# Sums of weight blocks by accumulating DMAs in place of VectorE, in a one-core hybrid attention and recurrence block

## The chip, the cores and the metric

The kernel runs on one core of a Trainium2 chip. The metric is device time in microseconds: the time of one launch of the whole program. The engines are named as the profile names them: PE is TensorE's matmul, PEld its loading of weights, DVE is VectorE, ACT is ScalarE, POOL is GpSimd and SP is SyncE. DMAs are started from the queue of SP (in a few places of ACT) and from the queue of POOL. Each queue runs its instructions in order.

## The reference

One layer of a decoder block on a sequence of 1024 tokens with 1024 channels, all in float32: a modulated RMSNorm, one wide input projection, two branches (sliding-window attention with 16 heads and 4 key heads, and a gated linear recurrence behind a short convolution), a gated merge of the two, an output projection, the residual and a last RMSNorm. Cut to what matters here:

```python
h = rmsnorm(x, norm_g[l]) * (1.0 + scale[:, None, :]) + shift[:, None, :]
proj = h @ w_in[l]
q, k, v, g_attn, xr, g_rnn, m_attn, m_rnn = jnp.split(proj, SPLIT_POINTS, axis=-1)
...
y_attn = sliding_window_attention_with_sinks(q, k, v, attn_sinks[l]) * jax.nn.silu(g_attn)
xr = causal_depthwise_conv(xr, conv_w[l], conv_b[l])
y_rnn = rg_lru(xr, positions, ...) * jax.nn.silu(g_rnn)
merged = (jax.nn.sigmoid(m_attn) * (y_attn @ w_attn_proj[l])
          + jax.nn.sigmoid(m_rnn) * (y_rnn @ w_rnn_proj[l]))
x = x + gate[:, None, :] * (merged @ w_out[l])
```

The change concerns `h @ w_in`, the largest product.

## The kernel before

**Precision.** Every float32 operand of a matmul is split in two float32r parts, a high part (a rounded copy, made on ACT) and a low part (what is left, made on DVE); a product is then three matmuls: high times high, low weight times high, high weight times low. In the names, `wh` and `wl` are the two parts of a block of weights, `hh`, `hl` those of the activations h, `nh`, `nl` those of differences of activations.

**Seven products for eight.** The output columns of `w_in` are cut in chunks of 128 and taken in 22 pairs of chunks (class `Pair`, line 700). The weights of a pair are four blocks of 128 by 512 numbers in memory: A11, A12 (first chunk, the two halves of the 1024 input channels) and A21, A22 (second chunk). The 2 by 2 block product is done with seven block products by Strassen's method in Winograd's form. It needs four sums of weight blocks: S1 = A21 + A22, S2 = S1 - A11, S3 = A21 - A11 and S4 = S2 - A12. S2 is made from S1 and S4 from S2. The other side needs four sums of activation blocks, made once (`differences`, line 563, then split by `make_operands`, line 571). Each product is 12 matmuls of 128 by 128 by 512 (`product`, line 691).

**Slots.** `run` (line 818) emits the products in slots. Pair i has its first slot at s = 7i; the products of a pair come at s (A11), s+1 (S1), s+3 (S2), s+4 (A12), s+5 (S4), s+6 (S3) and s+9 (A22, in the place between S1 and S2 of the next pair). Behind the product of slot t stand the steps that were put down for t in a table (`at_slot`, line 676): loads, sums, high parts (`hi`), low parts (`lo`), copies out of the accumulators and what is done with the results (the `sinks`). The background work (the gates of the recurrence, the preparation of `w_out` and so on) is fitted in between by `background` (line 653), with estimated costs of each step on ACT and DVE. The order on each engine is fixed when the program is built.

**Before the first pair** the steps of slots -6 to 0 are emitted at three places by hand (`begin`, lines 1559, 1578 and 1581), among the steps that finish the operands of the activations.

**Around the change, per pair.** At s-6 to s-4 SP loads A11 and A21, A22 and A12. The high and low parts and the four sums (`tsum`, line 715, on DVE) are put at s-2 to s+5; S1 at s-2, S2 at s-1, S3 at s, S4 at s+2. A22's parts follow at s+7. C11, C12, C21 and C22, the four result blocks, go to the sinks at s+5 to s+11: rotary embedding for q, a tanh for the gates, the convolution for the recurrence.

**POOL's queue** holds, in this stretch, only DMAs that prepare `w_out`: `out_weights` (line 1168) loads blocks `wq`, DVE multiplies and subtracts them, and POOL stores them to `wq_d`. When the last pair but one is nearly done, the attention is opened (`open_attn`, line 1234): SP loads keys, queries and the sinks of the softmax, POOL copies a column of the sinks into the first tile of scores, loads values, and from then on also stores the tanh results (`smr_d`) and does the masks. The last pair runs between the first steps of attention.

Of the kernel before, what the change touches and what calls it, by code (L numbers as in the profile page):

```python
# [22 lines left out]
P = 128  # L23
S = 1024
# [28 lines left out]
def tile_hybrid_block(ctx, tc, x, x_t, pk, rows, posr, posi, c_row, w_ss, w_gate, w_main, w_v,  # L53
# [8 lines left out]
    def f32(ap):  # L62
        return ap.bitcast(F32)
# [497 lines left out]
    NT1, NT3, NT4, T2 = [], [], [], []  # L561

    def differences(i):
# [3 lines left out]
        V.tensor_tensor(out=b12_, in0=b12_, in1=b22, op=ALU.subtract)  # L567
        V.tensor_tensor(out=b22, in0=b22, in1=b11, op=ALU.add)
        V.tensor_tensor(out=b21, in0=b21, in1=b22, op=ALU.subtract)

    def make_operands(i):
# [5 lines left out]
        NT3.append((nh[i][:, SL[1]], nl[i][:, SL[1]]))  # L577
        NT4.append((nh[i + 4][:, SL[0]], nl[i + 4][:, SL[0]]))
        T2.append((nh[i + 4][:, SL[1]], nl[i + 4][:, SL[1]]))
# [41 lines left out]
    def rope_b(src, th, dst, r0=P):  # L621
        t = {}

        def f1():
            t["h"] = rpp.tile([P, HALF], F32R, tag="rh", name="rhi", bufs=2)
            A.copy(t["h"][:], src())

        def f2():
            t["l"] = rpp.tile([P, HALF], F32R, tag="rl", name="rlo", bufs=2)
            V.tensor_tensor(out=t["l"][:], in0=src(), in1=f32(t["h"][:]), op=ALU.subtract)  # L630
# [69 lines left out]
    class Pair:  # L700
# [3 lines left out]
        def place(self, s, par, last, put_):  # L704
# [4 lines left out]

            def load(n):  # L710
                i, j = int(n[1]) - 1, int(n[2]) - 1
                return "S", 0, 0, lambda: R.__setitem__(
                    n, load_half(w_main[self.c + i][:, SL[j]]))

            def tsum(dst, a, b, op):
                def f():
                    R[dst] = wp.tile([P, HALF], F32, tag="ws", name="ws", bufs=3)[:]
                    V.tensor_tensor(out=R[dst], in0=R[a], in1=R[b], op=op)
                return "D", 0, 0.69, f
# [7 lines left out]
            def lo(n):  # L727
                return "D", 0, 0.69, lambda: rest(O[n], R[n], sc)

            SUB, ADD = ALU.subtract, ALU.add  # L730
            at_slot(s - 6, [load("A11"), load("A21")], load("A22"), load("A12"))
            put_(s - 2, [hi("A11"), tsum("S1", "A21", "A22", ADD)],
                 [hi("S1"), lo("A11"), tsum("S2", "S1", "A11", SUB)],
                 [lo("S1"), tsum("S3", "A21", "A11", SUB)],
                 hi("S2"),
                 [hi("A12"), lo("S2"), tsum("S4", "S2", "A12", SUB)],
                 [hi("S4"), lo("A12")], [hi("S3"), lo("S4")], lo("S3"))
            at_slot(s + (5 if last else 7), hi("A22"), lo("A22"))
# [14 lines left out]
            def join(out_, n, a, b):  # L753
# [1342 lines left out]
```

## Time and profile before

| what | before |
|---|---|
| time, three runs | 912.44, 913.25, 914.01 us; median 913.25 |
| profiled execution, span from first to last instruction | 910.2 us (its time outside the span is not recorded) |
| granted TensorE clock, mean | 0.997 |
| PE busy | 892.0 us, 98% of the span |
| DVE busy | 722.1 us, 79% |
| ACT busy | 557.6 us, 61% |
| POOL busy | 125.2 us, 14% |
| bytes moved by DMA | 182.05 MB, mean 200 GB/s |
| sums of weight blocks on DVE (line 718) | 88 of 128x512, 60.2 us in all |

The pairs run from 112 us to about 584 us of the span. Before that are the norm, the first products and the operands; after it the rest of the attention, the projections of the two branches, the merge and the output projection. A matmul of 128x512 is shown as 389 ns long, but matmuls are pipelined and one starts every 0.227 us, so that a slot of 12 is 2.73 us. Busy time of PE is the time in which at least one is under way.

### The profile page before, as it was taken

The numbers are of one execution on the slowest core, as the hardware profiler recorded it, in microseconds if no ns is written. First come the engines' busy times: TensorE is split into PE (matmuls) and PEld (weight loads), VectorE is DVE, ScalarE is ACT, GpSimd is POOL, SyncE is SP. The second block draws the span as 40 slices with busy tenths as digits, with TensorE's granted clock in tenths as the row PEclk, the third lists the DMA queues.
The fourth block names the chain that finished last, engine by engine and source line by source line (L and its number), as shares of the span: only waits on it lengthen the run. The fifth ranks groups of instructions, "written<-read, shape, count | busy, mean of one in ns | idle before, by whom it ended". The sixth has DMA issues, their size and how long they took to land.

```text
span 910.2 us, 12609 instructions
## 1 busy us (share of the span) xinstructions
PE 892.0 (98%) x4187; PEld 740.7 (81%) x4187; DVE 722.1 (79%) x1143; ACT 557.6 (61%) x1088; POOL 125.2 (14%) x204
## 2 busy tenths in 40 slices
PE   5999999999999999999999999999999999999997
PEld 3879888887888788888887888888888888888886
DVE  7976889797679983988498576899999946779875
ACT  6753655454566755775678685888888731114555
POOL 0120000000010010000000001354444421310002
PEclk9999999999999999999999999999999999999998
DMA  9963458862344362346155257996666259878314
GB/s 351 414 212 110 163 168 312 281 230 85 116 144 151 116 234 86 115 151 225 36 197 166 84 192 253 338 368 215 203 199 219 93 172 330 306 273 322 140 46 185
DMA packets 88598, 182.05 MB, mean 200 GB/s; under 512 B 13891, under 2 KB 30275, under 8 KB 88534
## 3 DMA queue, kind: packets, MB, share of 16 engines
q1 hardware_dynamic: 81908, 161.57, 51.0%
q0 software_dynamic: 6336, 19.37, 5.9%
q8 instruction: 33, 0.54, 0.2%
q14 instruction: 31, 0.25, 0.1%
q10 hardware_dynamic: 290, 0.32, 0.1%
HBM read 124.49 MB, written 57.12 MB: 200 GB/s over the span
## 4 chain that ended last, share of the span: by engine, by line
PE 87%; DVE 5%; DMA 4%; ACT 2%; issue 1%; POOL 0%; SPq 0%; DVEq 0%; ACTq 0%
PE bk L696 43%; PE rp L174 13%; PE bo L1869 7%; PE pmain L174 6%; PE pgate L991 5%; PE bk L174 3%; PE s_ps L1283 3%; PE pv L1355 2%; DMA r<-w_main 2%; PE pt L1321 1%; DVE wl L110 1%; PE bk L1529 1%; PE bk L1528 1%; PE bk L1527 1%; DMA wada<-w_ss 1%
## 5 line engine op out<-in xcount | busy, mean ns | idle before, releaser
L696 PE MATMUL bk<-nh,wl 128*128 128x512 f32 x352 | 137.4, 390 | 0.4 <-DVE wl L110 0.4
L696 PE MATMUL bk<-nh,wh 128*128 128x512 f32 x352 | 137.1, 389 | 0.0
L696 PE MATMUL bk<-nl,wh 128*128 128x512 f32 x352 | 137.0, 389 | 0.0
L110 DVE TENSOR_TENSOR wl<-r,wh 128x512 fp32r<-128x512 f32 x113 | 80.5, 727 | 7.4 <-ACT wh L104 7.4
L104 ACT CAST wh<-r 128x512 fp32r<-128x512 f32 x113 | 68.6, 618 | 21.6 <-PE bk L1529 12.2
L60 POOL DMA_DIRECT2D wq_d<-wq x32 | 22.0, 687 | 423.7 <-DVE wq L1181 379.3
L696 PEld LDWEIGHTS bk<-nh,wl 128*128 128x128 f32 x352 | 66.1, 188 | 15.1 <-DVE wl L110 1.5
L696 PEld LDWEIGHTS bk<-nh,wh 128*128 128x128 f32 x352 | 66.1, 188 | 13.8
L696 PEld LDWEIGHTS bk<-nl,wh 128*128 128x128 f32 x352 | 66.1, 188 | 13.6
L696 PE MATMUL bk<-hh,wl 128*128 128x512 f32 x176 | 68.6, 390 | 0.4 <-DVE wl L110 0.4
L696 PE MATMUL bk<-hh,wh 128*128 128x512 f32 x176 | 68.6, 390 | 0.0
L696 PE MATMUL bk<-hl,wh 128*128 128x512 f32 x176 | 68.5, 389 | 0.0
L110 DVE TENSOR_TENSOR wl<-ws,wh 128x512 fp32r<-128x512 f32 x76 | 51.7, 683 | 0.0
L1307 ACT ACTIVATE p<-p,small 128x129 f32<-128x129 f32 x128 | 50.1, 401 | 0.0
L104 ACT CAST wh<-ws 128x512 fp32r<-128x512 f32 x76 | 45.8, 614 | 0.1
L1869 PE MATMUL bo<-wh,sum 128*128 128x512 f32 x128 | 39.6, 389 | 0.0
L696 PEld LDWEIGHTS bk<-hh,wh 128*128 128x128 f32 x176 | 33.0, 188 | 7.7 <-ACT wh L104 0.9
L696 PEld LDWEIGHTS bk<-hh,wl 128*128 128x128 f32 x176 | 33.0, 188 | 7.5 <-DVE wl L110 0.8
L696 PEld LDWEIGHTS bk<-hl,wh 128*128 128x128 f32 x176 | 33.0, 188 | 6.9
L1283 PE MATMUL s_ps<-ks,qs 128*128 128x256 f32 (+1 forms) x256 | 37.6, 289 | 0.2 <-DVE p L1297 0.2
L799 ACT ACTIVATE c<-bk 128x512 f32<-128x512 f32 x29 | 17.3, 597 | 30.2 <-PE bk L696 30.2
L696 PE MATMUL bk<-hha,wl 128*128 128x512 f32 x88 | 34.5, 392 | 0.6 <-DVE wl L110 0.5
(412 smaller groups left out, 2336.7 us busy)
## 6 DMA issues: line engine op xcount, KB each, us to landing
r<-w_main SPq DMA_DIRECT2D x100, 256.0 KB, 4.3
wada<-w_ss SPq DMA_DIRECT2D x16, 512.5 KB, 9.0
qs<-q_d SPq DMA_DIRECT2D x16, 512.0 KB, 5.8
wq_d<-wq POOLq DMA_DIRECT2D x24, 256.0 KB, 4.6
wr<-wq_d SPq DMA_DIRECT2D x24, 256.0 KB, 5.0
ks<-k_d SPq DMA_DIRECT2D x24, 192.0 KB, 5.0
wq<-w_out POOLq DMA_DIRECT2D x16, 256.0 KB, 5.7
q_d<-rhi SPq DMA_DIRECT2D x16, 256.0 KB, 4.1
```

Source lines behind the costliest of these rows:

```text
L60: return eng.dma_start(dst, src)
L104: A.copy(dst[0][:], src)
L110: V.tensor_tensor(out=dst[1][:], in0=src, in1=f32(dst[0][:]), op=ALU.subtract)
L174: mm = T.matmul(ps[hf], ww, xx[kc][hf], start=(kc == 0 and ww is w_h and xx is xh), stop=(kc == KC - 1 and xx is xl))
L696: W["pe"] = T.matmul(ps, ww[:, c], b[kc][xx_], start=(first and kc == 0 and i == 0), stop=(kc == 3 and i == 2), skip_group_check=not first)
L799: A.activation(t["t"], s(), AF.Tanh, scale=0.5)
L991: W["pe"] = T.matmul(ps[:, SL[hf]], ww[:, c0:c0 + P], xx_[:, SL[hf]], start=(ic == 0 and i == 0), stop=(ic == 1 and i == 2))
L1283: W["pe"] = T.matmul(o, qs[:, j, qc], ks[:, b, k0 + (0 if n else P):k0 + 256], start=(b == 0), stop=(b == 1))
L1307: A.activation(px[:, j, :], px[:, j, :], AF.Exp, bias=sm[:, 0, j:j + 1], accum_out=sm[:, 1, j:j + 1])
L1321: W["pe"] = T.transpose(pt[:, j, :], px[:, j, 0:P], ident[:])
L1355: W["pe"] = T.matmul(pv[:], b, m[:].rearrange("p j q -> p (j q)"), start=(i == 0), stop=(i == len(prods) - 1))
L1869: T.matmul(bank[p][i] if dst is None else dst, a[:, ts_], b[:][:, sl], start=(new and kc == 0 and j == 0), stop=(kc == 3 and j == 2), skip ...
```

## The change

The four sums of a pair are made by DMAs that add what they read to what lies in the tile (`accum_op=ALU.add`), started from POOL's queue, `grow` in the diff. One tile X of the pool `ws` takes, one after the other, A21 (a plain load), then + A22 (this is S1), + A11 (S2), + A12 (S4). The tile that held A11 takes + A21 and becomes S3. Since a DMA can add but not subtract, the sums stand with the other sign where it was a difference: with -A21, -A22 as the second chunk's blocks all four sums are what the method needs times -1. Three of the four sums of activations are therefore taken with the other sign too, and the results of the second chunk come out negative and are turned in the sinks (a scale of -1 in an instruction that was there anyway).

Each block is now read from memory by each DMA that adds it: eight transfers of 256 KB per pair in place of four. A DMA that adds to X waits until the high and the low part of what X held have been made. The steps stand at other slots: A21 is loaded at s-8, S1 is made at s-6, A11 is loaded at s-6, A12 at s-2, A22 at s+3; S1's high part is at s-3 and its low part at s-2, with S2's DMA behind it; S2's parts at s and s+1, with S4's DMA behind; S4's parts at s+3 and s+4.

```diff
@@ -558,15 +558,17 @@
...
-    NT1, NT3, NT4, T2 = [], [], [], []
+    NT1, T3, T4, NT2 = [], [], [], []
 
     def differences(i):
         b11, b12_ = xT[i][:, SL[0]], xT[i][:, SL[1]]
         b21, b22 = xT[i + 4][:, SL[0]], xT[i + 4][:, SL[1]]
         V.tensor_tensor(out=b11, in0=b11, in1=b12_, op=ALU.subtract)
-        V.tensor_tensor(out=b12_, in0=b12_, in1=b22, op=ALU.subtract)
-        V.tensor_tensor(out=b22, in0=b22, in1=b11, op=ALU.add)
-        V.tensor_tensor(out=b21, in0=b21, in1=b22, op=ALU.subtract)
+        V.tensor_tensor(out=b12_, in0=b22, in1=b12_, op=ALU.subtract)
+        V.scalar_tensor_tensor(out=b22, in0=b22, scalar=-1.0, in1=b11, op0=ALU.mult,
+                               op1=ALU.subtract)
+        V.scalar_tensor_tensor(out=b21, in0=b22, scalar=-1.0, in1=b21, op0=ALU.mult,
+                               op1=ALU.subtract)
 
     def make_operands(i):
         for t in (i, i + 4):
...
@@ -618,16 +620,20 @@
         return [("AD", 1.16, 0.69, f1), ("D", 0, 1.38, f2)] + rope_b(
             lambda: t["ra"], th, dst, 0)
 
-    def rope_b(src, th, dst, r0=P):
+    def rope_b(src, th, dst, r0=P, sign=1.0):
         t = {}
 
         def f1():
             t["h"] = rpp.tile([P, HALF], F32R, tag="rh", name="rhi", bufs=2)
-            A.copy(t["h"][:], src())
+            if sign > 0:
+                A.copy(t["h"][:], src())
+            else:
+                A.activation(t["h"][:], src(), AF.Copy, scale=sign)
 
         def f2():
             t["l"] = rpp.tile([P, HALF], F32R, tag="rl", name="rlo", bufs=2)
-            V.tensor_tensor(out=t["l"][:], in0=src(), in1=f32(t["h"][:]), op=ALU.subtract)
+            V.scalar_tensor_tensor(out=t["l"][:], in0=src(), scalar=sign, in1=f32(t["h"][:]),
+                                   op0=ALU.mult, op1=ALU.subtract)
             dma(dst[r0:r0 + P, SL[th]], t["h"][:])
             dma(dst[r0 + 2 * P:r0 + 3 * P, SL[th]], t["l"][:])
 
@@ -707,16 +713,22 @@
             R, O, sc = {}, {}, self.scale
             self.ops, self.banks = O, (b1, b2, b3, bk[2 - par])
 
+            def part(n):
+                i, j = int(n[1]) - 1, int(n[2]) - 1
+                return w_main[self.c + i][:, SL[j]]
+
             def load(n):
-                i, j = int(n[1]) - 1, int(n[2]) - 1
-                return "S", 0, 0, lambda: R.__setitem__(
-                    n, load_half(w_main[self.c + i][:, SL[j]]))
-
-            def tsum(dst, a, b, op):
+                return "S", 0, 0, lambda: R.__setitem__(n, load_half(part(n)))
+
+            def begin_sum():
+                R["X"] = wp.tile([P, HALF], F32, tag="ws", name="ws", bufs=3)[:]
+                dma(R["X"], part("A21"))
+
+            def grow(dst, t, n):
                 def f():
-                    R[dst] = wp.tile([P, HALF], F32, tag="ws", name="ws", bufs=3)[:]
-                    V.tensor_tensor(out=R[dst], in0=R[a], in1=R[b], op=op)
-                return "D", 0, 0.69, f
+                    G.dma_start(R[t], part(n), accum_op=ALU.add)
+                    R[dst] = R[t]
+                return "N", 0, 0, f
 
             def hi(n):
                 def f1():
@@ -727,15 +739,19 @@
             def lo(n):
                 return "D", 0, 0.69, lambda: rest(O[n], R[n], sc)
 
-            SUB, ADD = ALU.subtract, ALU.add
-            at_slot(s - 6, [load("A11"), load("A21")], load("A22"), load("A12"))
-            put_(s - 2, [hi("A11"), tsum("S1", "A21", "A22", ADD)],
-                 [hi("S1"), lo("A11"), tsum("S2", "S1", "A11", SUB)],
-                 [lo("S1"), tsum("S3", "A21", "A11", SUB)],
-                 hi("S2"),
-                 [hi("A12"), lo("S2"), tsum("S4", "S2", "A12", SUB)],
-                 [hi("S4"), lo("A12")], [hi("S3"), lo("S4")], lo("S3"))
-            at_slot(s + (5 if last else 7), hi("A22"), lo("A22"))
+            def early(t, *steps):
+                at_slot(max(t, -6), *steps)
+
+            ADD, SUB, MUL = ALU.add, ALU.subtract, ALU.mult
+            early(s - 8, ("S", 0, 0, begin_sum))
+            early(s - 6, [grow("S1", "X", "A22"), load("A11")])
+            at_slot(s - 2, load("A12"))
+            at_slot(s + (1 if last else 3), load("A22"))
+            put_(s - 3, hi("S1"), [lo("S1"), grow("S2", "X", "A11"), hi("A11")],
+                 [lo("A11"), grow("S3", "A11", "A21")])
+            put_(s, hi("S2"), [lo("S2"), grow("S4", "X", "A12")], hi("A12"),
+                 [lo("A12"), hi("S4")], [lo("S4"), hi("S3")], lo("S3"))
+            at_slot(s + (5 if last else 7), [hi("A22"), lo("A22")])
 
             T_ = {}
 
@@ -750,17 +766,18 @@
             at_slot(s + 4, keep("u2", b2))
             at_slot(s + 5, *self.sinks["C11"](lambda: b1))
 
-            def join(out_, n, a, b):
+            def join(out_, n, a, b, sign=1.0):
                 def f():
                     T_[n] = out_()
-                    V.tensor_tensor(out=T_[n], in0=a(), in1=b(), op=SUB)
+                    V.scalar_tensor_tensor(out=T_[n], in0=a(), scalar=sign, in1=b(), op0=MUL,
+                                           op1=ADD if sign > 0 else SUB)
                 return "D", 0, 0.69, f
 
             d12, k12 = self.sinks["C12"]
             d22, k22 = self.sinks["C22"]
             at_slot(s + 6, join(d12, "C12", lambda: T_["u2"][:], lambda: b3),
                     *k12(lambda: T_["C12"]))
-            at_slot(s + 7, join(d22, "C22", lambda: b2, lambda: T_["p5"][:]),
+            at_slot(s + 7, join(d22, "C22", lambda: b2, lambda: T_["p5"][:], -1.0),
                     *k22(lambda: T_["C22"]))
             if last:
                 def add():
@@ -773,7 +790,7 @@
     def rope_q(g):
         return {"C11": lambda s: rope_a(s, 0, q_d[g]), "C12": (blk, lambda s: rope_a(
                     s, 1, q_d[g])),
-                "C21": lambda s: rope_b(s, 0, q_d[g]), "C22": (blk, lambda s: rope_b(
+                "C21": lambda s: rope_b(s, 0, q_d[g], sign=-1.0), "C22": (blk, lambda s: rope_b(
                     s, 1, q_d[g])), "late": 11}
 
     behind = []
@@ -790,24 +807,24 @@
             behind.pop(0)()
 
     def tanh_sinks(dst, silu):
-        def steps(j, th):
+        def steps(j, th, sign=1.0):
             def sink(s):
                 t = {}
 
                 def f1():
                     t["t"] = blk()
-                    A.activation(t["t"], s(), AF.Tanh, scale=0.5)
+                    A.activation(t["t"], s(), AF.Tanh, scale=0.5 if silu else 0.5 * sign)
                     if not silu:
                         dma(dst[j][:, SL[th]], t["t"], G if "att" in W else nc.sync)
 
                 def f2():
-                    V.scalar_tensor_tensor(out=t["t"], in0=t["t"], scalar=1.0, in1=s(),
+                    V.scalar_tensor_tensor(out=t["t"], in0=t["t"], scalar=sign, in1=s(),
                                            op0=ALU.add, op1=ALU.mult)
                     store(dst[j][:, SL[th]], t["t"])
 
                 return [("A", 0.62, 0, f1)] + ([("D", 0, 0.69, f2)] if silu else [])
             return sink
-        return {"C11": steps(0, 0), "C12": (blk, steps(0, 1)), "C21": steps(1, 0),
+        return {"C11": steps(0, 0), "C12": (blk, steps(0, 1)), "C21": steps(1, 0, -1.0),
                 "C22": (blk, steps(1, 1))}
 
     def place(pairs):
@@ -821,11 +838,11 @@
         for t in range(-6, 7 * n + 14):
             i, k = divmod(t, 7)
             q = {0: (0, "A11", B11, 1, True), 1: (0, "S1", NT1, 2, True),
-                 2: (-1, "A22", NT4, 1, False), 3: (0, "S2", T2, 1, False),
+                 2: (-1, "A22", T4, 1, False), 3: (0, "S2", NT2, 1, False),
                  4: (0, "A12", B21, 0, False), 5: (0, "S4", B22, 2, False),
-                 6: (0, "S3", NT3, 1, False)}[k]
+                 6: (0, "S3", T3, 1, False)}[k]
             if t == 7 * n:
-                q = -1, "A22", NT4, 3, True
+                q = -1, "A22", T4, 3, True
             d = 0.0
             if 0 <= i + q[0] < n and t <= 7 * n:
                 d = extra()
@@ -865,7 +882,8 @@
             return xr[ic]
 
         def copy(ic):
-            return lambda s: [("A", 0.58, 0, lambda: A.copy(row(ic)[:, SL[0]], s()))]
+            return lambda s: [("A", 0.58, 0, lambda: A.activation(
+                row(ic)[:, SL[0]], s(), AF.Copy, scale=-1.0 if ic else 1.0))]
 
         def half(ic):
             return lambda: row(ic)[:, SL[1]]
```

**How instructions move.** PE runs the same matmuls; those of the gates stand a few products earlier, since the planner counts DVE as freer. DVE loses the 88 sums, POOL gains 88 DMAs. Three places matter for the prediction.

On ACT, ahead of the first pair. `wh` from `r` is the high part of A11, `wh` from `ws` that of a sum, `nh` are high parts of activations, the `c` from `bk` are tanh results. Before:

```order
L106 ACTIVATE wh_1188<-r_1068 128x512
L1571 ACT_TABLE_LOAD
L1571 ACTIVATE c_1193<-bk2_70 128x512
L1571 ACTIVATE c_1196<-bk3_71 128x512
L574 CAST nh2_772<-xT_201 128x1024
L574 CAST nh6_773<-xT_205 128x1024
L106 ACTIVATE wh_1205<-ws_1191 128x512
L574 CAST nh3_770<-xT3_202 128x1024
L574 CAST nh7_771<-xT7_206 128x1024
```

and in the change, from the same place:

```order
L106 ACTIVATE wh_1185<-ws_1068 128x512
L106 ACTIVATE wh_1192<-r_1071 128x512
L1589 ACT_TABLE_LOAD
L1589 ACTIVATE c_1195<-bk2_70 128x512
L1589 ACTIVATE c_1198<-bk3_71 128x512
L576 CAST nh2_772<-xT_201 128x1024
L576 CAST nh6_773<-xT_205 128x1024
L106 ACTIVATE wh_1211<-ws_1068 128x512
L576 CAST nh3_770<-xT3_202 128x1024
L576 CAST nh7_771<-xT7_206 128x1024
```

S1's high part now stands ahead of A11's; the high part from `ws_1068` in the second place, between `nh6` and `nh3`, is S2's, which before was S1's (S2's came behind `nh7` and two more).

On SP, where the attention is opened. `ks`, `qs` and `sink` are its first loads, `smr_d` a store of a tanh result, `r` a load of weights. Before:

```order
L60 DMA r_5067<-w_main 128x512
L60 DMA smr_d4_118<-c_5103 128x512
L60 DMA ks_5129<-k_d_87 64x2x256 x2
L60 DMA qs_5132<-q_d0_98 128x4x256
L60 DMA sink_5126<-rows 128x16
L60 DMA ks_5136<-k_d_87 64x2x384 x2
```

and in the change:

```order
L60 DMA r_4981<-w_main 128x512
L60 DMA smr_d3_117<-c_5018 128x512
L60 DMA r_5021<-w_main 128x512
L60 DMA ks_5039<-k_d_87 64x2x256 x2
L60 DMA qs_5042<-q_d0_98 128x4x256
L60 DMA sink_5036<-rows 128x16
L60 DMA ks_5046<-k_d_87 64x2x384 x2
```

Before, the first load of keys stood behind the store of the first result of pair 21 of 22 (`smr_d4`, slot 145); now it stands behind the last result of pair 20 (`smr_d3`, slot 143), two slots earlier.

On POOL, at the same hand-over. `yh_d`, `yl_d` are the last results of the recurrence, `p` from `sink` is the first tile of scores, `dv` and `vs` are values. Before:

```order
L60 DMA yh_d7_129<-yh_5111 128x1024
L60 DMA yl_d7_137<-yl_5114 128x1024
L1271 COPY p_5127<-sink_5126 128x4
L60 DMA dv_5142<-dv_d0_93 128x256
L60 DMA vs_5141<-vs_d0_89 128x128
L60 DMA smr_d4_118<-c_5180 128x512
L60 DMA smr_d5_119<-c_5201 128x512
L1300 AFFINE_SELECT p_5127<-p_5127 128x4x128
```

and in the change, from the same `yh_d`, where `ws` and `r` from `w_main` are sums of the last pair:

```order
L60 DMA yh_d7_129<-yh_4983 128x1024
L60 DMA yl_d7_137<-yl_4986 128x1024
L1289 COPY p_5037<-sink_5036 128x4
L60 DMA dv_5052<-dv_d0_93 128x256
L60 DMA vs_5051<-vs_d0_89 128x128
L60 DMA smr_d4_118<-c_5089 128x512
L729 DMA ws_4933<-w_main 128x512
L729 DMA r_4981<-w_main 128x512
L60 DMA smr_d4_118<-c_5131 128x512
L60 DMA smr_d5_119<-c_5151 128x512
L729 DMA ws_4933<-w_main 128x512
L1318 AFFINE_SELECT p_5037<-p_5037 128x4x128
```

The DMAs that make S2 and S3 of the last pair stand behind the copy of the sinks, two loads of values and one store; S4's behind two stores more, and the mask of the first scores behind S4's.

6 lines of the change are left out of this document (3 added, 3 removed).

## The prediction

> **What bounds the kernel now.** I read three views first: busy time by engine, busy time by stretch, and PE's waits. Behind the times of the windows stand the number of instructions, then the granted clock, the DMA engines' mean busy share and GB/s.
>
> ```profile
> PE 892.0 (98%) x4187; PEld 740.7 (81%) x4187; DVE 722.1 (79%) x1143; ACT 557.6 (61%) x1088; POOL 125.2 (14%) x204
> core 0: us, PE busy (x) PEld busy (x) DVE busy (x) ACT busy (x) POOL busy (x), PEclk, DMA share, GB/s
> 45.00:112.00 67.00, 66.49 (x382) 58.25 (x381) 49.07 (x72) 35.02 (x55) 5.18 (x10) 1.00 0.47 168
> 112.00:566.00 454.00, 452.63 (x1989) 371.56 (x1989) 356.75 (x510) 291.73 (x426) 16.89 (x27) 1.00 0.48 165
> 566.00:896.00 330.00, 329.64 (x1633) 277.26 (x1632) 270.04 (x457) 192.18 (x539) 97.64 (x155) 1.00 0.67 232
> PE bk L387 <- DVE xt L381: 7.0, 1, 7.0
> PE bk L696 <- DVE wl L110: 1.3, 3, 0.5
> 112.27 106.17 PE bk L696 x467
> ```
>
> From 45 to 896 us PE is busy for 66.49 + 452.63 + 329.64 of 851 us: 2.2 us are idle. DVE's 79% is busy time beside it, not ahead of it. The largest wait (7.0 us) is at line 387, before the pairs, where the change touches nothing. The last row is from the chain of waits: 467 of the pairs' matmuls in 106.17 us without a break, so one takes 0.2273 us and a slot of 12 takes 2.73 us.
>
> **The change part by part.**
>
> *Removed: 88 sums on DVE.* From the groups by line:
>
> ```profile
> L718 DVE TENSOR_TENSOR ws<-r 128x512 f32<-128x512 f32 x44 | 30.1, 685 | 1.9 <-DMA r<-w_main 1.9
> L718 DVE TENSOR_TENSOR ws<-ws,r 128x512 f32<-128x512 f32 x44 | 30.1, 684 | 0.0
> ```
>
> 60.2 us of DVE go. PE can gain only where it waits for DVE: 1.3 us in three waits for low parts in the pairs (line 110). I count half, -0.6, since each such low part also needs a high part from ACT, which is relieved of nothing. Bounds: 0 and -1.3.
>
> *Added: 88 accumulating DMAs on POOL's queue.* No row shows such a DMA. What matters is L, the time from its issue to its landing, since each sum waits for the one before it. The nearest rows are POOL's own transfers (medians; the `wq` rows are from the windows 200 to 300, 300 to 400 and 400 to 500 us, `smr_d` and `yl_d` from 545 to 600; then the tile `wq` over the whole span), beside SP's load of the same block:
>
> ```profile
> r<-w_main SPq DMA_DIRECT2D x100, 256.0 KB, 4.3
> wq<-w_out POOLq DMA_DIRECT2D x2, 256.0 KB, 4.3
> wq<-w_out POOLq DMA_DIRECT2D x2, 256.0 KB, 5.9
> wq<-w_out POOLq DMA_DIRECT2D x2, 256.0 KB, 5.1
> smr_d<-c POOLq DMA_DIRECT2D x7, 256.0 KB, 6.4
> yl_d<-yl POOLq DMA_DIRECT2D x1, 512.0 KB, 7.5
> L60 POOL DMA_DIRECT2D wq_d<-wq x32: 565/727/744, 263.0 to 804.7; - x32
> DMA to landing us min/median/max: 2.0/4.7/9.4
> ```
>
> A load of 256 KB takes 4.3 to 5.9 us here. An accumulating one also reads its destination, so I take the largest, L = 5.9, for the pairs, and 6.4 where the attention opens. Bounds: 4.3 (the second stream costs nothing) and 7.5 (as much as 512 KB). The 22.5 MB more, over 454 us, add 50 GB/s to 165, still below the 232 of the next stretch. POOL's issues cost 88 times 0.73 = 64 us of an engine that has 16.89 busy in 454: hidden.
>
> The Trainium skill, "DMA: Bandwidth & Descriptors", section "Anatomy of one DMA — SWDGE (gpsimd) path", fits such a DMA by 2.0 us and its bytes at 436 GB/s; for 256 KB that is an estimate of 2.6 us. The trace's 4.3 to 5.9 do not agree, and no run here shows an accumulating one. By the page every loss below would vanish but the 0.3 of the first pair's low part, and the time would be 913.0.
>
> *The first pair.* It has no run-up. ACT's and DVE's timelines:
>
> ```profile
> 105.26 0.63 ACT L106 ACTIVATE wh<-r 128x512 fp32r<-128x512 f32 x1
> 108.17 2.00 ACT L574 CAST nh<-xT 128x1024 fp32r<-128x1024 f32 x2
> 110.59 2.00 ACT L574 CAST nh<-xT 128x1024 fp32r<-128x1024 f32 x2
> 113.44 0.65 ACT L106 ACTIVATE wh<-ws 128x512 fp32r<-128x512 f32 x1
> 106.00 0.69 DVE L718 TENSOR_TENSOR ws<-r 128x512 f32<-128x512 f32 x1
> 109.25 2.36 DVE L575 TENSOR_TENSOR nl<-xT,nh 128x1024 fp32r<-128x1024 f32 x2 [2.57 <-ACT nh L574]
> 111.53 0.68 DVE L112 SCALAR_TENSOR_TENSOR wl<-r,wh 128x512 fp32r<-128x512 f32 x1
> ```
>
> S1's high part now stands ahead of A11's on ACT: 0.63 later for the `nh` behind them, for the `nl` on DVE and for A11's low part at 111.53, which then ends at 112.84. PE takes the high parts first and wants it some 0.23 into the product, at 112.50: 0.34 late.
>
> The chain of sums: S1's low part takes the place of the sum at 106.00 and ends at 106.7. S2's DMA lands at 106.7 + 5.9 = 112.6; its high part (0.65) ends at 113.25. Ahead of its low part stand two `nh` (2.0) on ACT and the second `nl` half (1.2) on DVE: 116.45, and 117.1 with it. S4's DMA lands at 123.0, high part 123.65, low part 124.35. S4's product is the fifth: it starts at 112.27 + 0.34 + 4 x 2.73 = 123.5 and wants the low part at 123.75: 0.6 late. Together 0.9. Bounds: 0.34 at L = 4.3, and 0.3 + 3.8 = 4.1 at 7.5, since two transfers of the chain count.
>
> *The pairs between.* High parts of successive sums stand three slots apart, 8.2 us. Less a high part (0.65 us) and a low part (0.68) there remain 6.9 for L and for waiting in DVE's order: 5.9 fits, so nothing is lost. How far it may grow: from S1's high part (behind the product of slot s-3) to S4's product (s+5) are seven slots, 19.1 us. Three high parts and two low parts take 3.3, and of S4's low part 0.45 must lie ahead of the product; 15.4 remain for two transfers. So the loss starts at about L = 7.7 and is 2 x (L - 7.7) a pair beyond. This term is 0 at both bounds of L.
>
> *The hand-over to the attention.* From the timelines of SP, POOL, ACT and DVE and, for the last five rows, the chain of waits around 566 us:
>
> ```profile
> 555.76 0.39 SPq L60 DMA_DIRECT2D sink<-rows  x1
> 562.11 0.19 POOL L1271 COPY p<-sink 128x4 f32<-128x4 f32 x1 [5.52 <-DMA sink<-rows]
> 564.02 1.09 POOL L60 DMA_DIRECT2D smr_d<-c  x2
> 560.64 0.57 ACT L748 COPY bk<-bk 128x512 f32<-128x512 f32 x1 [0.86 <-PE bk L696]
> 564.68 0.62 ACT L104 CAST wh<-r 128x512 fp32r<-128x512 f32 x1
> 567.93 0.59 ACT L1291 COPY p<-s_ps 128x512 f32<-128x512 f32 x1 [2.14 <-PE s_ps L1283]
> 568.55 0.74 DVE L1297 COPY_PREDICATED p<-mgt,s_ps 128x512 f32<-128x512 uint32 x1 [0.86 <-ACT p L1291]
> 569.97 0.59 ACT L799 ACTIVATE c<-bk 128x512 f32<-128x512 f32 x1
> 564.11 2.83 PE bk L696 x12
> 566.94 0.95 PE s_ps L1283 x8
> 567.89 2.75 PE bk L696 x12
> 570.64 0.95 PE s_ps L1283 x8
> 574.78 0.95 PE s_ps L1283 x8
> ```
>
> POOL's queue is in order: the copy at 562.11 waits for the load of the sinks, and the last pair's S2 and S3 DMAs are queued behind it, two loads of values and a store. The first loads move two slots up on SP, 5.46 us. So S2's DMA is issued at 564.02 + 0.55 - 5.46 = 559.1 and lands at 565.5 (L = 6.4); its high part ends at 566.1. On ACT there follow a tanh and a copy of the pair's results (0.59 and 0.57), then the copy that empties the one buffer of scores (0.59): 567.9. PE's second scores, at 566.94, wait for that: 0.95 late. S2's low part (566.8) is in time for its product at 567.89. S4's DMA is issued behind it, 567.3, lands at 573.7; ACT's copy and DVE's masked copy of the third scores follow by 575.65, before the fourth scores at 574.78 + 0.95. So 1.0; bounds 0 (L = 4.3) and 3.1 (7.5, two transfers in part).
>
> *Sum.* -0.6 + 0.9 + 0 + 1.0 = +1.3. The profiled execution's span is 910.2; with the median's 913.25 that leaves 3.05 around it, which the change does not touch. The sum on the span is 911.5, on the median **914.5**.
>
> **The rivals.**
>
> *Clearly slower, the queue at the hand-over.* If the load of the sinks lands as late as now, because the earlier loads meet the recurrence's last results (`yl_d` took 7.5 us just there), S2's DMA is issued at 564.57 and lands at 571.0; the copy of the scores ends 1.75 + 0.6 later, 573.3, for scores wanted at 566.94: 6.4 in place of 1.0, **920**. It decides once the copy of the sinks runs later than about 557.5, 0.85 behind the 556.65 reckoned above, where its loss alone reaches 1.8. For it: four other things precede S2 in that queue, and the copy waited 5.52 us before. Against: SP is in order as well, and the keys' loads stand two slots up.
>
> *Clearly slower, long sums.* If L is 7.5, the same chain gives 4.1 at the start and 3.1 at the hand-over, 913.25 - 0.6 + 7.2 = 920. From 7.7 on every pair pays: at the slowest `wq`, 9.4, 3.4 us for each of some 20, 68 more, **988** or above. For it: reading two streams. Against: medians of 4.3 to 5.9.
>
> A lock would make the same loss: the start of a POOL DMA held up while DVE works. Held for a run like the 2.35 us at 109.25, L is 5.9 + 2.35 = 8.25: 1.1 for each of 20 pairs beside those 920, 942. Against it: POOL's issues took 565 to 744 ns throughout, beside a DVE that is busy for 357 of 454 us. The Trainium skill, "SBUF — State Buffer", section "SBUF: two separate sides", describes this lock for VectorE's two-port operations; that the narrow spread of issues would exclude it here is my reading, and no run shows it for an accumulating DMA.
>
> *Faster.* PE's whole idle time between 45 and 896 us is 2.2. If the DMAs are as quick as the quickest loads and all of the waits for DVE go, 913.25 - 2.2 = **911.0**. Against: 1.3 only is named as DVE's.
>
> **How the numbers follow.** Below 0.2% (1.8 us) this kernel's runs can't tell a change. The forecast, +1.3 with small losses and gains around it, holds 0.45 within 0.2%, and 0.10 for a sum just above it (its two losses have bounds that reach 4.1 and 3.1). The queue at the hand-over has 0.15, long sums 0.18 and the lock 0.04; faster has 0.08. So slower holds 0.10 + 0.15 + 0.18 + 0.04 = 0.47. The forecast's own range is 912.2 to 917. The whole range goes up to 922, past both rivals at 920 and short of the cases in which every pair pays (about 0.14), and leaves out half of the faster case below 912.2.
>
> **What would show it.** PE's busy time stays at 892 and its waits name what is late. DVE's falls by 60 us to some 662, POOL's grows by 60. The accumulating DMAs' median from issue to landing should be 5 to 6.4; if it is above 7.7, ACT's high parts wait for them in every pair and PE's rows of 106 us without a break are cut at every fifth product. Around 112 and 123 us PE waits 0.3 and 0.6 for low parts. Near 561 us the second scores wait about 1 us for ACT's copy; if the copy of the sinks on POOL is not near 556.6, the queue's rival holds. I am wrong if PE's idle time is in the 454 us of the pairs, or if it is unchanged and the time falls: then DVE's work had a price on PE that these views do not name.

## The result, and the profile after

The change made the kernel **slower**: 934.8 us median (932.3 to 937.35, four runs) against 913.23 (912.44 to 914.01), a ratio of 1.0236 with a 95% interval of 1.0213 to 1.0258. The prediction was 914.5 with a range up to 922. The profiled execution of the changed kernel has a span of 935.6 us, 25.4 more than before.

From the page after: busy time by engine, POOL's DMA queue (packets, MB, share of 16 engines' time), then the DMA issues with their median time to landing (SP's loads of weights, which took 4.3 before, and POOL's DMAs into `ws`). The last line is the tile `ws`, with least, median and most.

```profile
PE 901.9 (96%) x4187; PEld 742.2 (79%) x4187; DVE 673.9 (72%) x1055; ACT 558.4 (60%) x1088; POOL 201.8 (22%) x293
...
q0 software_dynamic: 19088, 42.71, 20.9%
...
r<-w_main SPq DMA_DIRECT2D x78, 256.0 KB, 5.9
ws<-w_main POOLq DMA_DIRECT2D x66, 256.0 KB, 6.5
...
DMA to landing us min/median/max: 3.0/6.5/10.3
```

The same queue on the page before:

```profile
q0 software_dynamic: 6336, 19.37, 5.9%
```

DVE did lose its sums. Its busy time falls by 48.2 us and not by their 60.2, mostly since instructions in a row overlap by some 0.08 us with each neighbour (the starts at 112.13 and 112.74 in the timeline before are 0.61 apart, at 0.68 each) and overlaps are counted once. PE does the same number of matmuls. What grew beyond expectation is the queue: 20.9% of 935.6 us less 5.9% of 910.2 us is 141.8 us of all sixteen engines, for 23.3 MB in 88 DMAs: **1.61 us of all sixteen engines for one DMA of 256 KB**.

Where the time went is read from the matmuls that PE gets done in a stretch. Windows of before, then of after (columns as in the prediction):

```profile
112.00:200.00 88.00, 87.90 (x388) 72.66 (x388) 75.82 (x141) 49.56 (x90) 0.00 (x0) 1.00 0.69 239
200.00:300.00 100.00, 100.00 (x438) 81.21 (x437) 78.57 (x108) 56.46 (x83) 4.20 (x6) 1.00 0.38 131
300.00:400.00 100.00, 99.09 (x436) 81.44 (x435) 78.60 (x106) 69.39 (x96) 4.21 (x6) 1.00 0.41 141
400.00:500.00 100.00, 99.64 (x438) 81.71 (x437) 81.49 (x105) 69.51 (x98) 4.20 (x6) 1.00 0.46 157
```

```profile
112.00:200.00 88.00, 80.80 (x338) 63.66 (x338) 58.54 (x110) 41.49 (x75) 14.80 (x17) 0.98 0.91 268
200.00:300.00 100.00, 98.59 (x428) 78.98 (x427) 67.96 (x96) 54.06 (x84) 29.72 (x38) 1.00 0.78 216
300.00:400.00 100.00, 98.13 (x424) 80.28 (x423) 71.34 (x88) 72.64 (x96) 17.72 (x21) 0.98 0.66 177
400.00:500.00 100.00, 99.28 (x434) 80.93 (x433) 74.75 (x94) 67.16 (x94) 24.19 (x30) 1.00 0.76 206
```

At 0.2273 us a matmul, 50 fewer from 112 to 200 us are 11.4 us; 10, 12 and 4 fewer in the next three stretches are 5.9. The remaining 8 us come behind 500 us. The stretch that lost most is the one whose DMA share was already 0.69 before; it is now 0.91.

Who was waited for, in ACT's waits after (total us, times, longest):

```profile
ACT wh L104 <- DMA ws<-w_main: 68.0, 29, 12.6
...
ACT wh L106 <- DMA ws<-w_main: 19.0, 6, 6.1
```

ACT stands 87 us, in 35 waits, at the high part of a sum whose DMA has not landed. Of these 6.5 us are waits for S1, 41.2 for S2 and 39.2 for S4 (by the order of the single records). The copies that free PE's accumulators stand behind these waits in ACT's order. One case is the first pair's S4, from the timelines of POOL, ACT and PE, with a window of the 3.4 us that follow:

```profile
116.64 1.76 POOL L729 DMA_DIRECT2D ws<-w_main  x2 [2.65 <-ACT bk L764]
124.89 0.63 ACT L106 ACTIVATE wh<-ws 128x512 fp32r<-128x512 f32 x1 [6.11 <-DMA ws<-w_main]
125.57 0.80 PE L702 MATMUL bk<-hh,wh 128*128 128x512 f32 x1 [1.97 <-ACT wh L106]
125.60:129.00 3.40, 3.40 (x7) 2.43 (x8) 1.43 (x3) 1.44 (x3) 0.00 (x0) 0.50 0.79 282
```

S4's DMA took 8.2 us; the forecast had 5.9. PE stood 1.97 us, and then ran at half its clock for 3.4 us. The other large case is the hand-over to the attention:

```profile
570.60 1.21 SPq L60 DMA_DIRECT2D sink<-rows  x1
576.66 0.19 POOL L1289 COPY p<-sink 128x4 f32<-128x4 f32 x1 [10.51 <-PE bk L702]
578.82 0.92 POOL L729 DMA_DIRECT2D ws<-w_main  x1
586.65 0.62 ACT L104 CAST wh<-ws 128x512 fp32r<-128x512 f32 x1 [12.57 <-DMA ws<-w_main]
588.22 0.58 ACT L1309 COPY p<-s_ps 128x512 f32<-128x512 f32 x1
PE s_ps L1301 <- ACT p L1309: 4.3, 1, 4.3
```

This is the chain that the prediction drew, step for step, with longer links: S2's DMA behind the copy of the sinks, its high part, a tanh and a copy, the copy of the scores, PE.

### The profile page after: what moved, and what is told of

The parts are those of the page before. It is cut to its first block, busy times and chain, and to the rows that moved or that the text cites. A ratio compares the mean times of both kernels' runs of the same rounds, so it can differ in the third digit from the quotient of the medians.

```text
span 935.6 us, 12755 instructions
## 1 busy us (share of the span) xinstructions
PE 901.9 (96%) x4187; PEld 742.2 (79%) x4187; DVE 673.9 (72%) x1055; ACT 558.4 (60%) x1088; POOL 201.8 (22%) x293
## 3 DMA queue, kind: packets, MB, share of 16 engines
q0 software_dynamic: 19088, 42.71, 20.9%
## 4 chain that ended last, share of the span: by engine, by line
PE 37%; DMA 14%; issue 8%; DVE 4%; ACT 3%; POOL 1%; SPq 1%; POOLq 0%; DVEq 0%; ACTq 0%
PE rp L174 12%; DMA ws<-w_main 7%; PE bo L1887 7%; PE bk L702 6%; PE pmain L174 5%; DMA hl<-yl_d 2%; PE s_ps L1301 2%; DMA yl<-yl_d 2%; PE pv L1373 2%; DVE wl L110 1%; PE pgate L1009 1%; PE pt L1339 1%; DMA hla<-yl_d 1%; ACT wh L104 1%; DMA qs<-q_d 1%
## 5 line engine op out<-in xcount | busy, mean ns | idle before, releaser
L729 POOL DMA_DIRECT2D ws<-w_main x66 | 58.4, 964 | 291.3 <-DVE wl L110 199.7
L110 DVE TENSOR_TENSOR wl<-r,wh 128x512 fp32r<-128x512 f32 x132 | 93.9, 722 | 22.8 <-ACT wh L104 22.7
L104 ACT CAST wh<-r 128x512 fp32r<-128x512 f32 x132 | 80.1, 617 | 36.1 <-PE bk L1547 12.2
L104 ACT CAST wh<-ws 128x512 fp32r<-128x512 f32 x57 | 35.3, 619 | 71.2 <-DMA ws<-w_main 68.0
L110 DVE TENSOR_TENSOR wl<-ws,wh 128x512 fp32r<-128x512 f32 x57 | 39.2, 687 | 40.1 <-ACT wh L104 40.1
```

The lines of the kernel that those rows point to most:

```text
L104: A.copy(dst[0][:], src)
L110: V.tensor_tensor(out=dst[1][:], in0=src, in1=f32(dst[0][:]), op=ALU.subtract)
L729: G.dma_start(R[t], part(n), accum_op=ALU.add)
```

## The experiments

Theory A: an accumulating DMA keeps the DMA engines busy about twice as long a byte as a load, so it lands late where they are busy, and the sums that wait for one another hold up ACT. Theory B: it is the moved order and the longer chain through POOL's queue, whatever the DMA does. All times below are medians, beside the kernel before on the same chip (912.4 to 912.8 us); "+" is the difference of the two medians. The ratios and their 95% intervals are of all executions and need not lie on the medians.

**Plain loads in place of the accumulating ones.**

```diff
-                    G.dma_start(R[t], part(n), accum_op=ALU.add)
+                    G.dma_start(R[t], part(n))
```

> The change with its 88 DMAs as plain loads of the same 256 KB (they overwrite the tile and add nothing, so the sums are left out); order, queue, bytes and dependences stay. Theory A (an accumulating DMA keeps the DMA engines busy about twice as long a byte, 10.3 GB/s an engine in the trace of the change against 22, lands late where the engines are full, and two in a row hold up the high parts on ScalarE): landing falls from 6.5 to 4.5-5.2 us, time 913 to 918. Rival B (the moved order and the longer chain through POOL's queue, whatever the DMA does): 928 or more, with the same waits at 125, 150, 190 and 589 us.

Measured: 918.8 us, +6.0 (ratio 1.0081, 1.0057 to 1.0104). POOL's queue and the largest waits of PE:

```profile
q0 software_dynamic: 13456, 42.71, 13.9%
...
ws<-w_main POOLq DMA_DIRECT2D x66, 256.0 KB, 4.8
...
PE s_ps L1301 <- ACT p L1309: 2.6, 1, 2.6
...
PE bk L702 <- DVE wl L110: 2.2, 2, 1.4
```

The same bytes from the same queue cost 13.9% of 916.5 less 53.7, 73.7 us of sixteen engines: 0.84 us a DMA, against 1.61. About 16 of the 21.6 us are the adding, 6 the rest of the change: both theories hold a part, and the time is a little above theory A's 913 to 918. Part of the price is in single packets: the most frequent one of an accumulating DMA carries 2 KB and takes 178 ns (median); a plain 2 KB packet takes 84. The plain loads of this run went out mostly in packets of 4 KB, 159 ns each, about as much time a byte as the plain packets of 2 KB.

**Half of the columns.**

```diff
-                    G.dma_start(R[t], part(n), accum_op=ALU.add)
+                    G.dma_start(R[t][:, 0:256], part(n)[:, 0:256], accum_op=ALU.add)
```

> The change with its DMAs adding only the first 256 of the 512 columns (half of each sum is left out). Theory A: engine time of the sums halves, landing some 4.8-5.5 us, time 916 to 923, near a plain load of the whole. Rival B: 928 or more. A variant of A in which an accumulating DMA has a long fixed time and its bytes do not matter: landing stays above 6 and time above 928.

Measured: 924.0 us, +11.2 (1.0097 to 1.0149): a little above the range given, but between the plain loads' 6.0 and the whole 21.6. An accumulating packet of 1 KB takes 102 ns, a plain one 46, so the factor of about two stands at both sizes. The engines' time falls with the bytes, to 14.5% of 922.1 us less 53.7, 80 us in place of 142, and the loss with it. But it is not the engines' time alone: the plain loads, with 73.7 us, lose 5 us less. What makes this difference is not shown.

**The last pair's sums on VectorE.** The slots and loads of before for that pair, with additions only:

```diff
+            if last:
+                at_slot(s - 6, [load("A11"), load("A21")], load("A22"), load("A12"))
+                put_(s - 2, [hi("A11"), tsum("S1", "A21", "A22")],
...
```

> The change with the sums of the last pair alone on VectorE, from loads and slots as before. If the hand-over to the attention costs what its one wait of 4.5 us and the small ones near it show: 934.8 less 5 to 6.5, 928 to 930. If the loss there only moves on to the next wait: 933 to 935.

Measured: 929.0 us, +16.2 (1.0157 to 1.022). That is 5.4 us less than the change's +21.6, give or take some 3.5 by the two intervals, and PE's wait of 4.3 us at the hand-over is gone: that loss comes with the last pair's DMAs and their slots.

**The first five pairs and the last on VectorE.** The same for `s < 35 or last`, with S2, S4 and S3 added in place.

> The change with the sums of the first five pairs (to about 207 us) and of the last one on VectorE, in place, at the slots of before; sixteen pairs keep the DMAs. If the losses stand where PE's gaps stand in the trace of the change (11 us more between 100 and 200 us, about 6 at the hand-over, 6 in between): 917 to 920. If the middle has room only because the start has already put PE late: the loss moves on, 923 or more.

Measured: 919.2 us, +6.8 (1.0043 to 1.0085). With the run before, the 21.6 us divide into 5.4 for the last pair, 9.4 for the first five and 6.8 for the sixteen others; by the intervals the first two are known to some 3.5 us, the third to some 2. The first five pairs, a quarter of them, run where the DMA share was 0.69 without any accumulation.

**S1 and S3 by DMA, S2 and S4 on VectorE.**

```diff
-            put_(s - 3, hi("S1"), [lo("S1"), grow("S2", "X", "A11"), hi("A11")],
+            put_(s - 3, hi("S1"), [lo("S1"), add("S2", "X", "A11"), hi("A11")],
...
-            put_(s, hi("S2"), [lo("S2"), grow("S4", "X", "A12")], hi("A12"),
+            put_(s, hi("S2"), [lo("S2"), add("S4", "X", "A12")], hi("A12"),
```

> The change with S1 and S3 still made by accumulating DMAs (44 of 256 KB), but S2 and S4 on VectorE, in place, in the same slots. S1 and S3 have slots to spare and no sum waits for a sum's DMA on the way from S1 to S4. Theory A in its form 'the chain of two is late': 913 to 916. If the traffic of accumulating DMAs counts, on the chain or off it: half of the 16 us that accumulating costs, 920 to 926.

Measured: 916.25 us, +3.8 (1.0023 to 1.0053), just above the chain theory's range. Without the chain, 44 accumulating DMAs are nearly free, though they take the engines as long (14.1% of 915.3 us less 53.7, 75 us) as the 88 plain loads. ACT's waits for a sum fall from 35 to 2.

**The mirror: S2 and S4 by DMA.**

```diff
+            early(s - 6, [load("A11"), load("A21")])
+            early(s - 5, load("A22"))
+            early(s - 4, ("D", 0, 0.69, first))
...
```

> The mirror of it: S2 and S4 by accumulating DMAs (44 of 256 KB), S1 and S3 on VectorE; the same bytes as in the run with S1 and S3 by DMA. The chain theory: most of the loss stays, 922 to 930, waits of ScalarE for ws and the wait of about 4 us at the hand-over in place. The traffic theory: the same as with S1 and S3, 920 to 926 for both.

Measured: 958.6 us, +46, far outside of what either theory gave. The reason is in the experiment. From DVE's waits:

```profile
DVE ws L741 <- DMA r<-w_main: 75.7, 18, 8.0
```

A22's load stood only a slot ahead of S1's sum, and DVE stood at that sum for 76 us. The run says nothing on the chain; it was made again below.

**S1's DMA a slot earlier.**

```diff
-            early(s - 8, ("S", 0, 0, begin_sum))
-            early(s - 6, [grow("S1", "X", "A22"), load("A11")])
+            early(s - 9, ("S", 0, 0, begin_sum))
+            early(s - 7, grow("S1", "X", "A22"))
+            early(s - 6, load("A11"))
```

> The change with S1's DMA (and the load before it) a slot earlier, so that it no longer starts right behind the DMA of the pair before that makes S4 (in the trace of the change the two were started 0.5 us apart and took 7 to 10 us). If two accumulating DMAs side by side make S4 late: S4's falls to about 6, time 926 to 931. If the other loads do it: 933 to 936.

Measured: 941.1 us, +28.7, worse than the change. In the change S4's DMA is started first and S1's, which has time, right behind it; S4's landed in 6.5 us (median) and S1's in 7.8. Moved ahead, S1's landed in 6.1 and S4's in 6.9. The one that is started second is the slower one both times, but 0.4 us more on S4's does not explain 7 us. ACT's waits for sums grow from 87 to 100 us, all of them for S2 and S4; why is not shown. Both answers of the expectation were wrong.

**The traffic without the chain.** The purest form, the kernel before with 88 such DMAs into a spare tile that nothing reads, has no time: there is no room for that tile in the on-chip memory. In its place: S2 and S4 on VectorE as above, with two more accumulating DMAs a pair at the phases of the change, into a tile that is done with:

```diff
+                at_slot(s + 5, idle_add("A11"))
+                at_slot(s + 8, idle_add("A12"))
```

> The kernel with S2 and S4 on VectorE, and on top of it two more accumulating DMAs of 256 KB in each pair but the last, into the tile of the pair whose S4 has been split already, at the slots (modulo seven) where the change starts those of S2 and S4; nothing waits for them. So the traffic of the change is there (86 of 88 DMAs) and the chain of two is not. Chain theory: 916 to 920, at most 3 us above the 916.25 without them. Traffic theory (engines full of accumulating packets slow every load and with it PE): 926 to 935.

Measured: 921.7 us, +9.0 (1.008 to 1.0117), between the two theories. Its queue shows that the traffic is really that of the change:

```profile
q0 software_dynamic: 18800, 42.18, 21.4%
...
r<-w_main SPq DMA_DIRECT2D x78, 256.0 KB, 5.5
...
ws<-w_main POOLq DMA_DIRECT2D x64, 256.0 KB, 6.3
```

So 5.2 us of the loss (+9.0 less +3.8) come with the traffic of these DMAs alone, and 12.6 (+21.6 less +9.0) need the chain. In numbers of matmuls from 112 to 200 us: before 388, this run 375, the change 338, although the DMA share is 0.97 here and 0.91 in the change.

**S2 and S4 by DMA, with early loads.**

```diff
+            early(s - 8, load("A21"))
+            early(s - 7, load("A22"))
...
+            at_slot(s + (1 if last else 5), load("A22"))
```

> S2 and S4 by accumulating DMAs, S1 and S3 on VectorE, with A21 and A22 loaded two to three slots ahead of S1's sum (in the earlier run of this kind VectorE stood 76 us waiting for the loads of S1). The chain of two at half the accumulating traffic. Chain theory: waits of ScalarE for ws and of the scores at the hand-over stay, 920 to 930, above the 916.25 of the run with S1 and S3 by DMA. Traffic theory: the same as that run, 915 to 918.

Measured: 936.9 us, +24.2: as slow as the change, with half of its accumulating DMAs, and above the range given. ACT's waits:

```profile
ACT wh L104 <- DMA ws<-w_main: 46.4, 21, 5.4
...
ACT wh L104 <- DMA r<-w_main: 24.8, 8, 8.6
```

The second line is a wait that the change has hardly at all (2.1 us for all loads of `r` from `w_main`): the late load of A22. What is the chain's and what is this load's, the last two runs tell.

**The other signs alone.** All sums on VectorE, at the slots of before:

> All 22 pairs with sums on VectorE at the slots of before; of the change only the other sign is left (three sums of activations, the sinks of the second chunk). Same instructions and the same durations: 912 to 914 by every theory. If the scalar_tensor_tensor forms or the negated copies cost something on VectorE or ScalarE that PE feels, 915 or more.

Measured: 912.65 us, ratio 0.9999 (0.999 to 1.0009). The signs cost nothing that shows.

**The chain a slot earlier, and the last pair on VectorE with it.**

```diff
+            early(s - 9, ("S", 0, 0, begin_sum))
+            early(s - 7, grow("S1", "X", "A22"))
...
+            put_(s - 4, hi("S1"), [lo("S1"), grow("S2", "X", "A11")], hi("A11"),
+                 [hi("S2"), lo("A11"), grow("S3", "A11", "A21")],
+                 [lo("S2"), grow("S4", "X", "A12")])
```

> The change with the same DMAs, but the chain of the sums (load of A21, S1's DMA and parts, S2's DMA and parts, S4's DMA) a slot, 2.73 us, earlier in each pair; S4's parts and all products stay, so S4's DMA has a slot more to land. Chain theory: in the change S4's high parts came one to two us late for PE, so most of the losses of the first and the middle pairs go and the hand-over's 5.8 stay: 918 to 925. If the chain only moves the loss to S1's or S2's DMA, which now start sooner after their loads: 930 or more.

> The same with the sums of the last pair on VectorE at the slots of before, which took 5.8 us off the change: 5 to 6.5 us under the run with the chain a slot earlier, 913 to 919. If the losses are not additive, less than 3 us under it.

Measured: 951.6 us (+39.3) and 942.7 (+30.4). The chain theory's 918 to 925 was missed by 27 us; the time lies in the other answer, 930 or more. The second expectation missed with the first: the last pair gave 8.9 in place of 5 to 6.5. The largest new stall is at neither S1's nor S2's DMA. PE stands 5.7 us, and the timelines of SP and DVE of the first of the two show for what:

```profile
497.29 0.33 SPq L60 DMA_DIRECT2D gg<-sgr_d  x1
...
505.15 1.23 DVE L1075 TENSOR_TENSOR rz<-rz,gg 128x1024 f32<-128x1024 f32 x1 [4.50 <-DMA gg<-sgr_d]
506.30 1.28 DVE L905 SCALAR_TENSOR_TENSOR xc<-xr,pk_t,xc 128x1022 f32<-128x1022 f32 x1
507.49 0.69 DVE L110 TENSOR_TENSOR wl<-r,wh 128x512 fp32r<-128x512 f32 x1
```

Another load (`gg`, for the recurrence) is late, and a low part of weights stands two places behind the instruction that waits for it. The change waits for these loads as well (8.5 us in 5 waits, before 0.8 in one), but no such stall of PE came of it. Is it the slots, or the accumulating packets?

**Both with plain loads** (the edit of the first experiment):

> The chain a slot earlier, with plain loads (the sums are left out). If the accumulating packets cause its 39 us over the kernel before: as the change with plain loads or below, 914 to 920. If the slots cause them: 935 or more.

> S2 and S4 by plain loads in place of accumulating DMAs (these two sums are left out), S1 and S3 on VectorE, A22 loaded late. If the accumulating packets on the chain cause its 24 us: 914 to 920. If the late load of A22 and the slots do: 928 or more.

Measured: 925.95 us (+13.3) and 924.5 (+11.8), between the answers. In the first, the same instruction waits 3.48 us for `gg` with plain loads too:

```profile
488.75 1.23 DVE L1075 TENSOR_TENSOR rz<-rz,gg 128x1024 f32<-128x1024 f32 x1 [3.48 <-DMA gg<-sgr_d]
```

So the slots and the plain transfers cost 12 to 13 us there, 6 to 7 more than in the change, and the adding costs the rest: 15.6 us in the change (+21.6 less +6.0), 12.4 with S2 and S4 alone, 26 with the chain a slot earlier. S2 and S4 by themselves, in slots of their own, thus cost most of what the adding costs for all four. Each of these differences is known to some 2 to 4 us.

## Why the prediction was wrong, point by point

**"I take the largest, L = 5.9".** It was taken from plain transfers, on the argument that an accumulating one "also reads its destination", and the bound of 7.5 was the landing of one transfer of twice the size. Over all DMAs into `ws` it measured 6.5 and 10.3 at worst, for all sums from 112 to 200 us 7.2. But the forecast's sum goes by the two transfers of the chain. In the single records these are 5.0 for S2 and 6.5 for S4 at the median, and 11.8 for the two of a pair, as much as twice 5.9; the slow ones are S1's, 7.8, which have time. That the size fits there is luck. As plain loads the two took 3.8 and 4.8, so the choice was too high for a load and allowed too little for the adding. Where single transfers counted it was too small: 8.2 for S4 of the first pair, 7.7 for S2 at the hand-over. By the page of the Trainium skill that the prediction weighed ("DMA: Bandwidth & Descriptors", section "Anatomy of one DMA — SWDGE (gpsimd) path") it would be 2.6, an estimate; the trace does not agree, for loads or sums.

**"Add 50 GB/s to 165, still below the 232".** This step counted bytes where engine time counts. Twice the time a byte makes the added load of the stretch 142 us of sixteen engines over 454 us, 0.31 of them, on 0.48. It also took one mean for a stretch that is not uniform: the share was 0.69 from 112 to 200 us and about 0.4 behind it. Read by 100 us, the windows before show the stretch that had the least room. SP's loads of weights beside the sums landed in 5.9 us at the median where they had taken 4.3.

**The pairs between, 0.** This is the step whose mechanism failed. The room of 6.9 us "for L and for waiting in DVE's order" left 1.0 for the waiting, and the margin beyond it ("the loss starts at about L = 7.7", 15.4 us for two transfers) left none. In the trace the two landings took 9.7 to 14.8 us, in none of the 22 pairs 15.4, and still ACT waited 35 times. From the start of S1's high part to that of S4's it took 18.9 us at the median. Landings are 11.8 of them and the parts made in between 2.6; the rest, more than 4 us, is waiting of parts and DMAs in the order of ACT, DVE and POOL. So ACT had done what stands ahead of S2's high part 4.1 us behind the start of S2's DMA (median), and 5.6 us for S4, where 6.9 were reckoned. The third pair, from S2's DMA to S4's high part:

```profile
150.04 0.86 POOL L729 DMA_DIRECT2D ws<-w_main  x1 [8.89 <-DVE wl L110]
157.84 0.61 ACT L104 CAST wh<-ws 128x512 fp32r<-128x512 f32 x1
160.84 0.68 DVE L110 TENSOR_TENSOR wl<-ws,wh 128x512 fp32r<-128x512 f32 x1
162.05 1.77 POOL L729 DMA_DIRECT2D ws<-w_main  x2 [5.91 <-ACT rhi L629]
168.54 0.62 ACT L104 CAST wh<-ws 128x512 fp32r<-128x512 f32 x1 [3.92 <-DMA ws<-w_main]
```

S2's DMA landed at 157.69. Its low part stood behind other work of DVE until 160.84, and S4's DMA started at 162.05: 4.4 us behind the landing, of which the two parts are 1.3. In time the pairs cost about 9 us in the first five (the first one's share included) and 6.8 in the sixteen others, and the slower loads beside the sums are 5.2 of the 21.6 without any chain.

**The first pair, 0.9.** The place was right and the size was not: A11's low part was 0.6 us late (forecast 0.34), S4's high part about 2 us (forecast: low part 0.6), from L = 8.2 beside loads of gate weights in the same 2 us. (The prediction took 112.27 for the start of A11's product; its first matmul stands at 111.78 in the timeline before.)

**The hand-over, 1.0.** The chain of instructions was right, and its cost was 5.4 by the run with the last pair's sums on VectorE. By then everything ran 18 us late: SP's first keys went out at 566.13, against 553.55 less 5.46 before. With these 18 us the copy of the sinks was due at 562.11 - 5.46 + 18 = 574.65; it ran at 576.66, 2.0 later, since SP took 4.5 us from the first keys to the load of the sinks, where it had taken 2.2. (The row names a matmul for the copy's wait; it ended 0.03 us behind the landing of the sinks at 576.53.) And S2's DMA took 7.7 in place of 6.4. The forecast's 0.95 with these 2.0 and 1.3 is PE's wait of 4.3: the rival of the queue gave 2.0 of it, that of the long sums 1.3.

**The gain, -0.6.** Nothing of it can be seen. The signs alone, with all sums on VectorE, are at 0.9999, and no run was clearly faster than the kernel before.

**What was left out: the price of a stall.** The sum counted a stall as its own length. Three stalls in the change were each followed by 3.4 us of half clock, some 1.6 us more for each.

Of the rivals, the long sums came nearest: its 920 to 988 holds the result, and what spoke for it, "reading two streams", is what the packets' times show (178 ns for 84). The way it reckoned to that time did not occur: it lets every pair pay from L = 7.7 on, and the landings on the chain were 5.0 and 6.5. That its range holds the result is in part luck. The engines' time for the second stream was in no term of the sum. The lock was not needed: with plain loads in the same queue most of the loss went.

What stays open: which stall comes first where the engines are nearly full was not forecast. The runs that moved slots (S1's DMA, the chain, the loads) missed their expectations by 5 to 29 us; in some a late load was seen behind it, and for S1's DMA the reason is not known. The division into chain (12.6) and traffic (5.2) rests on one kernel each, and in the run without the chain VectorE makes S2 and S4. How much of the chain's part is the longer landing and how much the waiting in order was not varied by itself: the plain loads shorten the one and leave the other, and lose 6.0.

## What to carry to other kernels

Cost a DMA in time of the DMA engines, not in bytes, and lay it on the share of each stretch of 100 us, not on the mean: an accumulating transfer took twice the engine time of a load here. In a chain through several engines, count for each link the wait in its engine's order, from the trace, before calling the rest a margin. Work that leaves an engine with room (VectorE had 21% idle and PE waited for it 1.3 us) for transfers in a chain buys nothing and puts two landings in front of an in-order queue. If sums are to be made by DMA, take those that nobody waits for soon: S1 and S3 alone cost 3.8 us in place of 21.6.

## What the runs showed of the hardware that was not expected

- An accumulating packet of 2 KB takes 178 ns where a plain one takes 84, and one of 1 KB 102 where a plain one takes 46. POOL's issue takes longer too: 873 ns at the median for the DMAs into `ws`, 538 for the same DMAs as plain loads.
- After a stall PE's clock can halve. From the traces of all these kernels, between 100 and 870 us: after 36 stalls of 1.0 to 1.73 us the granted clock stayed at 1.00; of 31 stalls from 1.80 us up, 24 came with 3.4 or 6.8 us at 0.50, which began between 2.5 us before the end of the stall and 2.1 us behind it, with a matmul every 0.427 us in place of 0.227. In 3.4 us eight matmuls start, which take 1.8 us at the full clock, so a stall of 2 us costs some 3.6, an estimate. The Trainium skill, "TensorE: Matmul & The Clock Gate", Part 1, puts the step down after about one idle window of 3.4 us, on a window that runs freely. The pieces of 3.4 us agree with that window; the stalls did not need to be that long.
